# Splitting the mixers' weights a turn later and ending it earlier, with the mixers' parts in a new order

## The chip, the cores and the metric

The kernel runs on one core of a Trainium2 chip. The metric is the device time of one execution in microseconds (us); with several runs their median is taken. The profile and the trace come from one execution of their own. TensorE is called PE in the rows, its weight loads PEld, VectorE DVE, ScalarE ACT, GpSimd POOL and SyncE SP.

## What is computed

The kernel computes a model of two layers over 512 positions of width 1024, in float32. Each layer is a feed-forward block (FFN), a mixer of three kinds of heads, and a second FFN; a final norm ends it:

```python
for l in range(DEPTH):
    x = x + 0.5 * swiglu(rmsnorm(x, ffn1_norm[l]), ffn1_w_gate[l], ffn1_w_up[l], ffn1_w_down[l])
    h = rmsnorm(x, mix_norm[l])
    p_a, p_b, p_c = _split(h @ w_in[l], (A_IN, B_IN, C_IN))
    ...
    o_a = rwkv7_mixer(r, k, v, w_lo, a_lo, g_lo, ...)
    o_b = dsa_mixer(q_b, c_b, iq_b, ik_b, iw_b, ...)
    o_c = retention_mixer(q_c, k_c, v_c, g_c)
    x = x + jnp.concatenate([o_a, o_b, o_c], axis=-1) @ w_out[l]
    x = x + 0.5 * swiglu(rmsnorm(x, ffn2_norm[l]), ffn2_w_gate[l], ffn2_w_up[l], ffn2_w_down[l])
return rmsnorm(x, final_norm)
```

`rmsnorm` divides x by the root of its mean square and multiplies by a gain. `rwkv7_mixer` is a recurrence over time with six heads of 64, `dsa_mixer` an attention over the 128 keys that an index picks for each query, `retention_mixer` a chunked linear attention with four heads. The FFN's inner width is 2752, `w_in` has 3400 columns (3416 in the second layer).

## The kernel before

**The precision.** A float32 product is made of three matmuls in the rounded format fp32r: each operand is split into a high and a low part, and high times high, low times high and high times low are summed in PSUM (`mm3`, lines 846 to 851). For a weight tile (128 x up to 8 x 128) `_weights` issues a load on SP's queue into `raw` (L783), a cast to `hi` on ACT (L787) and a subtraction to `lo` on DVE (L788). There are two buffers each of `raw`, `hi` and `lo`.

**The FFN.** `ffn` (line 904) takes x transposed, in eight tiles `x` of 128 features x 512 positions that stay in SBUF. The norm makes `gxh` and `gxl` of each tile (x times the gain, split; L866 on ACT and L867 on DVE), its squares (L877 on ACT), adds them on DVE (L882 and L886) and takes the sum over the partitions with one matmul, `ms` (L888). 43 tiles of the gate and up weights follow (`gu_tile`, 24 matmuls each), and in three groups eight tiles each of the down weights (`down`); a group's `down` stands after the first pair of the next group, the last group's at the end. Each `down` tile ends with an addition to the tile of x on DVE (L976).

**The ahead splits.** The mixers' weights `win` and `wout` are split during the FFNs before them. `ahead` (L792) takes one granule of 128 x 4 x 128: a load on POOL's queue (`later`, L816), which is issued once the cast of the weight tile in hand is done; a cast on ACT (`ahh`, L798), a subtraction on DVE into the loaded tile (`ahr`, L800), and two writes to DRAM on POOL's queue (L802). Both tiles come from the eight buffers of tag "ds". The first FFN of layer 0 has 54 such granules, its second and the first of layer 1 have 35 each, the last FFN none. An FFN has 43 + 24 = 67 turns, one per weight tile, and `other` spreads the granules over turns 9 to 67. The first FFN of each layer also loads the small weights after its fifth pair.

**The mixer.** `mix` (line 997) does not issue its operations at once. It records them in a `Stage`, which places them with a list scheduler by the dependencies, the free buffers, its own costs and the numbers in `TUNE`: `BIAS` and `FACTOR` shift and scale the urgency of each stream of operations, `DENSE` and `STICK` are two numbers of PE's choice, and `ORDER` is the order in which the blocks are recorded (rw0 to rw2 are the recurrence's pairs of heads, idx and att the attention's index and body, ret the retention, lat the keys' latent). Operations are then issued in the order found, and PE, DVE, ACT and POOL keep it; all of them carry line 1027. The mixer begins with a norm like the FFN's; each projection (`in`, 24 matmuls from `gxh`, `gxl` and the split weight tile `w`, loaded on SP's queue) is multiplied by `rb`, the inverse root that comes from `ms`, when it leaves PSUM. The recurrence inverts a triangular matrix with chains of 32x32 matmuls (`W` and `dX`). The `out` matmuls with `wout` end the mixer.

**The end.** In the last FFN the last `down` is done for one half of the positions and then the other, and `final` makes a norm of each half.

Of the kernel before, what the change touches and what calls it, by code (L numbers as in the profile page):

```python
# [19 lines left out]
NGU = 43  # L20
# [495 lines left out]
class Net:  # L516
# [9 lines left out]
            BIAS={"norm": -574, "in:lo": 168, "evac:in:lo": 94, "in:idx": 189, "evac:in:idx": 62,  # L526
                  "win-ret:cg0": -436, "evac:win-ret:cg0": 25, "win-ret:cg1": 55,
                  "evac:win-ret:cg1": 178, "rw": -349, "win-idx:iq0": -144, "evac:win-idx:iq0":
                  1039, "win-idx:iq1": -369, "evac:win-idx:iq1": 721, "win-idx:iq2": -63,
                  "evac:win-idx:iq2": 407, "win-idx:iq3": -76, "evac:win-idx:iq3": 431, "idx": 5,  # L530
                  "topk:1": 36, "topk:2": -524, "topk:3": -79, "win-ret:cq0": -30,
                  "evac:win-ret:cq0": 94, "win-ret:ck0": 47, "evac:win-ret:ck0": 311, "win-ret:cq1":
                  296, "evac:win-ret:cq1": 290, "win-ret:ck1": 389, "evac:win-ret:ck1": -2,
                  "win-ret:cv0": -35, "evac:win-ret:cv0": 420, "win-ret:cv1": 268,
                  "evac:win-ret:cv1": 282, "ret:in": 349, "ret:mid": 178, "ret:y": -40, "win-rw:k0":
# [8 lines left out]
                  "win-att:c": -97, "evac:win-att:c": 442, "lat": 64, "win-att:q0": -245,  # L544
                  "evac:win-att:q0": 507, "win-att:q1": -183, "evac:win-att:q1": 818, "win-att:q2":
                  -395, "evac:win-att:q2": 472, "att:0": 150, "att:1": 59, "att:2": -126, "out:oc":
                  -460, "wout:oc": -1030, "out:oa": -141, "wout:oa": -708, "out:ob": -332,
                  "wout:ob": -306},
            FACTOR={"norm": 0.83, "in:lo": 0.22, "evac:in:lo": 1.3, "in:idx": 1.65, "evac:in:idx":
# [29 lines left out]
            RETPS="pd",  # L579
            OUTPS="pi",  # L580
            AHEAD=2,
            DENSE=3013,
            STICK=5,
        ),
        dict(
# [53 lines left out]
            RETPS="pd",  # L639
            OUTPS="pi",  # L640
            AHEAD=1,
            DENSE=2209,
            STICK=13.5,
        ),
    )
# [1265 lines left out]
```

## Time and profile before

| | us |
|---|---|
| median of 3 runs | 2237.72 (2233.5 to 2244.03) |
| the profiled execution's own time | 2234.96 |
| its span, first to last instruction | 2233.0 |
| PE busy in it | 2141.7 |
| first FFN of layer 0, to PE's last `dn` matmul | 373.3 |
| mixer of layer 0 | 373.3 to 764.3 |
| the two FFNs between the mixers | 764.3 to 1118.3 and 1118.3 to 1474.5 |
| mixer of layer 1 | 1474.5 to 1860.4 |
| last FFN and final norm | 1860.4 to 2233.0 |

A row of the profile names the line, the engine, the operation and the tiles it writes and reads. The brackets of a timeline row tell how long the engine had been idle before it and which instruction or DMA ended that. The granted clock is that of TensorE as a share of its full speed; its mean over the span is 0.987. A window's busy time for PE says how much of a stretch PE had a matmul running, whatever the clock.

### The profile page before, as it was taken

How to read it: one execution, taken by the hardware profiler on the slowest of the kernel's cores; microseconds unless marked ns; L12 is line 12 of the kernel's file. 1: busy time of each engine (PE TensorE's matmuls, PEld its weight loads, DVE VectorE, ACT ScalarE, POOL GpSimd, SP SyncE). 2: the span in 40 equal slices, each digit the busy share in tenths (PEclk: the TensorE clock that was granted, in tenths of full speed). 3: DMA queues.
4: the chain of work that ended last, by engine and by line, in shares of the span. 5: the costliest groups of instructions: out<-in, count | busy, mean ns of one | idle time of the engine just before them, and what ended most of it. 6: DMA issues, size and time to landing. Idle time of an engine off the chain costs nothing.

```text
span 2233.0 us, 34747 instructions
## 1 busy us (share of the span) xinstructions
PE 2141.7 (96%) x13896; PEld 1735.7 (78%) x13896; DVE 1252.6 (56%) x2150; ACT 853.0 (38%) x1416; POOL 320.3 (14%) x549
## 2 busy tenths in 40 slices
PE   8999998999999899999999999989999989999997
PEld 6887876777677688888878888868777867888887
DVE  5545455359885554454555454543788735434446
ACT  4423335432455332332443232433435544322225
POOL 0322223121110011111201111211201100000001
PEclk9999998999999999999999999999999999999999
DMA  4766667333310445555535555574522113233224
GB/s 136 250 225 223 219 229 265 104 132 130 101 43 22 141 146 173 188 182 186 186 133 186 183 185 188 168 238 174 169 90 73 31 57 120 95 98 100 96 85 151
DMA packets 112290, 329.44 MB, mean 148 GB/s; under 512 B 15632, under 2 KB 32160, under 8 KB 112128
## 3 DMA queue, kind: packets, MB, share of 16 engines
q1 hardware_dynamic: 81056, 225.31, 30.3%
q0 software_dynamic: 31072, 101.90, 13.8%
q8 instruction: 109, 1.79, 0.3%
q14 instruction: 53, 0.43, 0.1%
HBM read 252.97 MB, written 72.09 MB: 146 GB/s over the span
## 4 chain that ended last, share of the span: by engine, by line
PE 47%; issue 32%; POOL 8%; DMA 7%; DVE 3%; ACT 3%; SPq 0%; POOLq 0%; DVEq 0%; ACTq 0%
PE in L1027 11%; PE gu L849 6%; PE gu L851 6%; PE gu L850 6%; POOL win L802 4%; PE out L1027 3%; DMA w<-win 3%; POOL ahr L816 2%; PE dn L851 2%; PE dn L849 2%; PE dn L850 2%; DMA w<-wout 2%; PE W L1027 1%; PE S L1027 1%; DMA ahr<-win 1%
## 5 line engine op out<-in xcount | busy, mean ns | idle before, releaser
L849 PE MATMUL gu<-gxh,hi 128*128 128x512 f32 x1376 | 539.2, 392 | 15.3 <-ACT hi L787 15.3
L851 PE MATMUL gu<-gxh,lo 128*128 128x512 f32 x1376 | 539.1, 392 | 2.6 <-DVE lo L788 2.6
L850 PE MATMUL gu<-gxl,hi 128*128 128x512 f32 x1376 | 537.6, 391 | 0.0
L787 ACT CAST hi<-raw 128x1024 fp32r<-128x1024 f32 (+3 forms) x292 | 282.6, 975 | 478.6 <-PE gu L850 221.6
L788 DVE TENSOR_TENSOR lo<-raw,hi 128x1024 fp32r<-128x1024 f32 (+3 forms) x292 | 329.6, 1134 | 61.2 <-ACT hi L787 54.5
L849 PEld LDWEIGHTS gu<-gxh,hi 128*128 128x128 f32 x1376 | 259.9, 189 | 72.1 <-ACT hi L787 17.9
L851 PEld LDWEIGHTS gu<-gxh,lo 128*128 128x128 f32 x1376 | 259.4, 189 | 60.4 <-DVE lo L788 6.3
L850 PEld LDWEIGHTS gu<-gxl,hi 128*128 128x128 f32 x1376 | 259.7, 189 | 54.8 <-issue 0.7
L851 PE MATMUL dn<-hh,lo 128*128 128x512 f32 (+1 forms) x712 | 269.1, 379 | 2.8 <-DVE lo L788 2.4
L849 PE MATMUL dn<-hh,hi 128*128 128x512 f32 (+1 forms) x712 | 269.1, 379 | 1.6 <-ACT hi L787 1.6
L850 PE MATMUL dn<-hl,hi 128*128 128x512 f32 (+1 forms) x712 | 268.6, 377 | 0.1
L1027 PE MATMUL in<-gxh,w 128*128 128x512 f32 (+1 forms) x736 | 250.5, 414 | 13.8 <-DMA w<-win 7.0
L800 DVE TENSOR_TENSOR ahr<-ahr,ahh 128x512 fp32r<-128x512 f32 x124 | 85.8, 692 | 308.7 <-ACT ahh L798 308.5
L798 ACT CAST ahh<-ahr 128x512 fp32r<-128x512 f32 x124 | 77.0, 621 | 354.1 <-DMA ahr<-win 255.0
L1027 PEld LDWEIGHTS in<-gxh,w 128*128 128x128 f32 x736 | 136.4, 191 | 52.2 <-DMA w<-win 12.2
L851 PEld LDWEIGHTS dn<-hh,lo 128*128 128x128 f32 x712 | 133.8, 188 | 31.3 <-DVE lo L788 7.0
L849 PEld LDWEIGHTS dn<-hh,hi 128*128 128x128 f32 x712 | 133.8, 188 | 29.0 <-ACT hi L787 5.0
L850 PEld LDWEIGHTS dn<-hl,hi 128*128 128x128 f32 x712 | 133.9, 188 | 25.0 <-DVE hl L856 0.3
L1027 PE MATMUL in<-gxl,w 128*128 128x512 f32 (+1 forms) x368 | 137.6, 408 | 0.6 <-DVE gxl L1027 0.6
L976 DVE SCALAR_TENSOR_TENSOR x<-dn,x 128x512 f32<-128x512 f32 (+1 forms) x104 | 67.0, 647 | 112.9 <-PE dn L851 112.2
L946 DVE TENSOR_TENSOR h<-gu,rb 128x512 f32<-128x512 f32 x84 | 57.9, 689 | 117.0 <-PE gu L851 116.9
L941 DVE TENSOR_TENSOR t<-gu,rb 128x512 f32<-128x512 f32 (+1 forms) x88 | 60.7, 689 | 92.0 <-PE gu L851 91.4
(328 smaller groups left out, 2744.1 us busy)
## 6 DMA issues: line engine op xcount, KB each, us to landing
raw<-wgu SPq DMA_DIRECT2D x172, 512.0 KB, 3.7
w<-win SPq DMA_DIRECT2D x92, 512.0 KB, 4.4
raw<-wdn SPq DMA_DIRECT2D x64, 512.0 KB, 3.5
ahr<-win POOLq DMA_DIRECT2D x92, 256.0 KB, 3.2
win<-ahh POOLq DMA_DIRECT2D x92, 256.0 KB, 2.4
win<-ahr POOLq DMA_DIRECT2D x92, 256.0 KB, 2.5
w<-wout SPq DMA_DIRECT2D x64, 192.0 KB, 2.6
raw<-wdn SPq DMA_DIRECT2D x24, 384.0 KB, 4.2
```

The costliest lines, as they stand in the source:

```text
L787: self.cast = nc.scalar.copy(hi[:, k:e], raw[:, :e - k])
L788: nc.vector.tensor_sub(lo[:, k:e], raw[:, :e - k], hi[:, k:e].bitcast(F32))
L798: nc.scalar.copy(hi, raw)
L800: nc.vector.tensor_sub(lo, raw, hi.bitcast(F32))
L802: nc.gpsimd.dma_start(d[:, k:k + 4], t)
L849: mm(ps, hi[:, k, :], rh, start=start, stop=False)
L850: mm(ps, hi[:, k, :], rl, start=False, stop=False)
L851: mm(ps, lo[:, k, :], rh, start=False, stop=stop)
L941: nc.vector.tensor_mul(t[:rows], g[:rows], rb[:rows])
L946: nc.vector.tensor_mul(h[:rows], u[:rows], rb[:rows])
L976: nc.vector.scalar_tensor_tensor(out=x, in0=ps, scalar=0.5, in1=x, op0=ALU.mult, op1=ALU.add)
L1027: op.ins = getattr(getattr(self.nc, op.engine), name)(*args, **kw)
```

## The change

It has four parts.

1. **The ahead splits.** A turn no longer loads a granule and casts it. It casts, subtracts and writes the granule that an earlier turn loaded, and then issues the load of the next. The cast is made to follow the cast of the weight tile in hand. The granules are spread over turns 6 to 59 of 67 (`NGU + 2 * NC`), so that the last `down` of eight tiles has none; with 54 granules that is one in each turn, with 35 it is 0.65 a turn (0.59 before).
2. **The mixers' tables.** All numbers of `BIAS` and `FACTOR`, `DENSE` and `STICK` are others, and `ORDER` is another, in both layers.
3. **The start.** In the first FFN of layer 0 the cast of the second weight tile is made to follow the sixth `gxh`.
4. **The end.** In the final norm of each half the last square is not added on DVE; a second matmul adds it in PSUM.

```diff
             ...
-            ORDER=("idx", "ret", "rw0", "rw1", "rw2", "lat", "att"),
+            ORDER=("rw0", "idx", "rw1", "ret", "lat", "rw2", "att"),
             ...
-            DENSE=3013,
-            STICK=5,
+            DENSE=1603,
+            STICK=23.4,
             ...
-    def ahead(self, l, n, m, k):
+    def ahead(self, item=None):
         nc = self.nc
         with self.kind(3):
-            for k in (k,):
-                raw, hi = self.z("ahr", shape=(128, 4, 128), tag="ds"), self.z("ahh", F32R, (128, 4, 128), "ds")
-                self.later(raw, self.a[n][l, :, m, k:k + 4])
-                nc.scalar.copy(hi, raw)
+            if self.loaded:
+                raw, (l, n, m, k) = self.loaded
+                hi = self.z("ahh", F32R, (128, 4, 128), "ds")
+                self.follow(nc.scalar.copy(hi, raw), self.cast)
                 lo = raw.bitcast(F32R)
                 nc.vector.tensor_sub(lo, raw, hi.bitcast(F32))
                 for t, d in zip((hi.bitcast(F32), raw), self.parts[l][n, m]):
                     nc.gpsimd.dma_start(d[:, k:k + 4], t)
+                self.loaded = None
+            if item:
+                l, n, m, k = item
+                raw = self.z("ahr", shape=(128, 4, 128), tag="ds")
+                self.later(raw, self.a[n][l, :, m, k:k + 4])
+                self.loaded = raw, item
 ...
             ins = nc.scalar.activation(hi, self.x[c], AF.Copy, scale=g)
+            self.early.append(ins)
 ...
-    def rms(self, ts, after=None):
+    def rms(self, ts, after=None, apart=False):
             ...
-            else:
+            elif c < NC - 1 or not apart:
                 nc.vector.tensor_add(acc, acc, sq)
         ps = self.ps("ms")[:, ts]
-        nc.tensor.matmul(ps, self.c("onesd"), acc, start=True, stop=True)
+        nc.tensor.matmul(ps, self.c("onesd"), acc, start=True, stop=not apart)
+        if apart:
+            nc.tensor.matmul(ps, self.c("onesd"), sq, start=False, stop=True)
 ...
-        skip = 8
-        step, done = len(ahead) / (NGU + 3 * NC - skip), [-skip * len(ahead) / (NGU + 3 * NC - skip), 0]
+        skip, step, turn, done = 5, len(ahead) / (NGU + 2 * NC - 5), [0], [0]
+        assert step <= 1
 
         def other():
-            done[0] += step
-            while done[1] < round(done[0]):
-                self.ahead(*ahead[done[1]])
-                done[1] += 1
+            turn[0] += 1
+            if turn[0] > skip and done[0] < min(len(ahead), round((turn[0] - skip) * step)):
+                self.ahead(ahead[done[0]])
+                done[0] += 1
+            elif done[0] == len(ahead):
+                self.ahead()
 ...
             w = self.weights(wgu[l, :, m], 8)
+            if self.phase == 1 and m == 1:
+
+                self.follow(self.cast, self.early[5])
             other()
 ...
-                rbs.append(self.rms(ts))
+                rbs.append(self.rms(ts, apart=True))
```

Two further lines let a `wout` tile be left out of the ahead splits where `LATE` names it; it names none in either version, so they change nothing. Line numbers move by one (L787 is L788 after) to 17 (L1027 is L1044).

On ACT, at the border of the first FFN and the first mixer, the instructions stood like this (`hi` is the cast of a weight tile of the last `down`, `ahh` that of a granule, `sq` and `gxh` belong to the mixer's norm, `x_72` is the first tile of x and `x_74` the second):

```order
L787 CAST hi_2851<-raw_2849 128x768
L787 CAST hi_2883<-raw_2881 128x768
L798 CAST ahh_2856<-ahr_2855 128x512
L787 CAST hi_2915<-raw_2913 128x768
L798 CAST ahh_2888<-ahr_2887 128x512
L787 CAST hi_2947<-raw_2945 128x768
L798 CAST ahh_2920<-ahr_2919 128x512
L798 CAST ahh_2952<-ahr_2951 128x512
L1027 ACTIVATE sq_2993<-x_72 128x512
L1027 ACTIVATE gxh_2977<-x_72,vec 128x512
L1027 ACTIVATE sq_2994<-x_74 128x512
```

After the change:

```order
L788 CAST hi_2854<-raw_2852 128x768
L1044 ACTIVATE gxh_2977<-x_72,vec 128x512
L1044 ACTIVATE sq_2993<-x_72 128x512
L788 CAST hi_2879<-raw_2877 128x768
L788 CAST hi_2904<-raw_2902 128x768
L788 CAST hi_2929<-raw_2927 128x768
L788 CAST hi_2954<-raw_2952 128x768
L1044 ACTIVATE gxh_2979<-x_74,vec 128x512
L1044 ACTIVATE sq_2994<-x_74 128x512
L1044 ACTIVATE gxh_2981<-x_76,vec 128x512
L1044 ACTIVATE sq_2995<-x_76 128x512
```

The four granule casts are gone from this stretch, and the norm's first rows stand among the last weight casts.

On DVE at the same place, before (the addition to `x_86`, the last tile of x, and the norm's `gxl` and sums of squares):

```order
L800 TENSOR_TENSOR ahr_2951<-ahr_2951,ahh_2952 128x512
L976 SCALAR_TENSOR_TENSOR x_86<-dn_2958,x_86 128x512
L1027 SCALAR_TENSOR_TENSOR gxl_2978<-x_72,vec,gxh_2977 128x512
L1027 SCALAR_TENSOR_TENSOR sq_2993<-sq_2994,sq_2993 128x512
L1027 SCALAR_TENSOR_TENSOR gxl_2980<-x_74,vec,gxh_2979 128x512
L1027 TENSOR_TENSOR sq_2993<-sq_2993,sq_2995 128x512
```

and after it, from the sixth of the norm's rows on to its last sum:

```order
L1044 SCALAR_TENSOR_TENSOR gxl_2984<-x_78,vec,gxh_2983 128x512
L993 SCALAR_TENSOR_TENSOR x_86<-dn_2958,x_86 128x512
L1044 TENSOR_TENSOR sq_2993<-sq_2993,sq_2996 128x512
L1044 SCALAR_TENSOR_TENSOR gxl_2986<-x_80,vec,gxh_2985 128x512
L1044 TENSOR_TENSOR sq_2993<-sq_2993,sq_2997 128x512
L1044 SCALAR_TENSOR_TENSOR gxl_2988<-x_82,vec,gxh_2987 128x512
L1044 TENSOR_TENSOR sq_2993<-sq_2993,sq_2998 128x512
L1044 TENSOR_TENSOR sq_2993<-sq_2993,sq_2999 128x512
L1044 SCALAR_TENSOR_TENSOR gxl_2990<-x_84,vec,gxh_2989 128x512
L1044 TENSOR_TENSOR sq_2993<-sq_2993,sq_3000 128x512
```

Before, all of the norm's rows stand behind the addition to the last tile of x, which stands behind the split of a granule; after, six of them stand ahead of it and eight behind it up to the last sum.

On PE, in the inverse of layer 1's second recurrence, the rows after the change read like this (`dX` and `W` are the inverse's chains, `rsc` and `kt` small matmuls of the retention):

```order
L1044 MATMUL rsc_12923<-sw_12913,ck_2829_12894 128x128 x3
L1044 MATMUL dX_12854<-W_12851,X_12850 32x32 x32
L1044 MATMUL rsc_12923<-sw_12913,ck_2829_12894 128x128
L1044 MATMUL rsc_12925<-qz_12914,ck_2829_12894 128x128 x3
L1044 MATMUL W_12855<-X_12850,G_12833 32x32 x2
L1044 MATMUL W_12855<-X_12850,G_12834 32x32 x2
```

Before, the corresponding rows have projections (`in`) and products of the attention (`K`, `V`) between the chains:

```order
L1027 MATMUL K_13118<-cT_13040,wuk_10348 128x512
L1027 MATMUL K_13053<-cT_13040,wuk_10348 128x512
L1027 MATMUL dX_12828<-W_12825,X_12824 32x32 x32
L1027 MATMUL V_13060<-wuv_10350,cT_13040 128x128 x3
L1027 MATMUL W_12829<-X_12824,G_12807 32x32 x2
L1027 MATMUL W_12829<-X_12824,G_12808 32x32 x2
```

The chains are the same 32x32 matmuls; what lies between them has moved from 512-wide to 128-wide ones.

More of the change, by code (lines that the diff above doesn't have):

```diff
@@ L525 @@
         dict(
[L526 to L535, printed above, removed]
[8 rows of a table removed]
[L544 to L548, printed above, removed]
@@ L549 @@
-            FACTOR={"norm": 0.83, "in:lo": 0.22, "evac:in:lo": 1.3, "in:idx": 1.65, "evac:in:idx":
[18 rows of a table removed]
-                    1.84, "win-att:c": 0.2, "evac:win-att:c": 0.82, "lat": 0.2, "win-att:q0": 8.07,
-                    "evac:win-att:q0": 0.89, "win-att:q1": 1.57, "evac:win-att:q1": 2.62,
-                    "win-att:q2": 0.42, "evac:win-att:q2": 1.18, "att:0": 1.03, "att:1": 0.21,
-                    "att:2": 2.71, "out:oc": 0.2, "wout:oc": 2.02, "out:oa": 0.33, "wout:oa": 5.32,
-                    "out:ob": 0.2, "wout:ob": 3.44},
@@ L609 @@
-            FACTOR={"norm": 0.58, "in:lo": 7.83, "evac:in:lo": 0.23, "in:idx": 10.01, "evac:in:idx":
[18 rows of a table removed]
-                    1.68, "win-att:c": 0.61, "evac:win-att:c": 0.23, "lat": 2.22, "win-att:q0":
-                    1.89, "evac:win-att:q0": 0.23, "win-att:q1": 3.17, "evac:win-att:q1": 0.23,
-                    "win-att:q2": 1.73, "evac:win-att:q2": 0.23, "att:0": 2.76, "att:1": 1.73,
-                    "att:2": 1.01, "out:oc": 21.13, "wout:oc": 1.43, "out:oa": 0.2, "wout:oa": 4.45,
-                    "out:ob": 0.22, "wout:ob": 8.85},
@@ L633 @@
-            ORDER=("idx", "ret", "rw0", "rw1", "rw2", "lat", "att"),
+            BIAS={"norm": -1505, "in:lo": 403, "evac:in:lo": 1676, "in:idx": 354, "evac:in:idx":
[14 rows of a table added]
+                  550, "ret:mid": 436, "ret:y": 153, "win-att:c": 1, "evac:win-att:c": 151, "lat":
+                  455, "win-rw:k2": -527, "evac:win-rw:k2": 908, "win-rw:v2": -402,
+                  "evac:win-rw:v2": 3075, "win-rw:r2": -493, "evac:win-rw:r2": 2546, "rw2": 326,
+                  "rw2:in": -117, "rw2:gram": -19, "rw2:inv": -217, "rw2:state": 633, "rw2:y": 311,
+                  "win-att:q0": -165, "evac:win-att:q0": 1549, "win-att:q1": -434,
+                  "evac:win-att:q1": 1232, "win-att:q2": -312, "evac:win-att:q2": 1097, "att:0": 30,
+                  "att:1": -52, "att:2": -202, "out:oc": -992, "wout:oc": -1924, "out:oa": -161,
+                  "wout:oa": -1162, "out:ob": -834, "wout:ob": -1488},
@@ L634 @@
+            ORDER=("rw0", "idx", "rw1", "ret", "lat", "rw2", "att"),
             LATE=(),
@@ L641 @@
             AHEAD=1,
-            DENSE=2209,
-            STICK=13.5,
+            DENSE=2838,
+            STICK=113.3,
         ),
@@ L760, in setup @@
                        for n, k in (("win", NWIN), ("wout", NC)) for m in range(k)
-                       if n == "wout" or WIN_ORDER[m] not in self.TUNE[l]["LATE"]} for l in range(L)]
-        self.smalls = {}
+                       if (WIN_ORDER[m] if n == "win" else n) not in self.TUNE[l]["LATE"]} for l in range(L)]
+        self.smalls, self.loaded, self.early = {}, None, []
     def c(self, name):
@@ L1153, in _mix @@
             for m in range(NC):
-                w = self.split_weights(l, "wout", m, k0, kt)
+                if ("wout", m) in self.parts[l]:
+                    w = self.split_weights(l, "wout", m, k0, kt)
+                else:
+                    w = self.weights(a["wout"][l, :, m, k0:k0 + kt], kt)
                 if gi == 0:
```

50 lines of the change are left out of this document (38 added, 12 removed), and 103 rows, old and new, of tables (BIAS, FACTOR).

## The prediction

> **What bounds the kernel now.** I read the busy times first, then the stages by windows, then the waits and the timeline at the borders of the stages.
>
> ```profile
> span 2233.0 us, 34747 instructions
> PE 2141.7 (96%) x13896; PEld 1735.7 (78%) x13896; DVE 1252.6 (56%) x2150; ACT 853.0 (38%) x1416; POOL 320.3 (14%) x549
> ```
>
> TensorE (PE) is busy for 2141.7 of 2233.0 us: 91.3 us of idleness and the stretches at a low clock are all that a change of order can win. The windows say where they lie. The columns are start:end and length, then busy time and count on PE, PEld, DVE, ACT and POOL, the granted clock, the DMA share and GB/s.
>
> ```profile
> 7.00:113.00 106.00, 103.92 (x437) 83.71 (x438) 61.61 (x80) 46.99 (x66) 18.86 (x35) 1.00 0.57 191
> 157.00:246.00 89.00, 87.39 (x385) 71.68 (x384) 46.66 (x60) 33.20 (x45) 23.75 (x45) 1.00 0.67 220
> 373.30:764.30 391.00, 355.23 (x3769) 278.20 (x3770) 261.10 (x589) 170.59 (x363) 47.88 (x68) 0.97 0.31 103
> 764.30:1118.30 354.00, 353.36 (x1553) 290.81 (x1552) 182.45 (x227) 128.27 (x165) 57.29 (x106) 1.00 0.52 173
> 1474.50:1860.40 385.90, 357.75 (x3775) 281.74 (x3774) 254.41 (x595) 166.90 (x363) 45.63 (x64) 0.97 0.33 111
> ```
>
> The mixers (373.3 to 764.3 and 1474.5 to 1860.4) hold 391.00 − 355.23 = 35.8 us and 385.90 − 357.75 = 28.2 us of PE's idleness, 64 of 91. The second FFN of layer 0 holds 0.6 us though it splits 35 granules ahead; the first, with 54, loses 2.1 and 1.6 us in the two windows shown. So the FFNs are PE's own work, and what can move lies in the mixers, at their borders and in the first FFN.
>
> The border of the first FFN and the mixer, from the timeline (start, length, instruction, and in brackets the idle time before it and what ended it):
>
> ```profile
> 365.79 0.84 ACT L787 CAST hi<-raw 128x768 fp32r<-128x768 f32 x1
> 370.37 0.62 ACT L798 CAST ahh<-ahr 128x512 fp32r<-128x512 f32 x1 [3.75 <-DMA ahr<-wout]
> 374.66 0.62 ACT L798 CAST ahh<-ahr 128x512 fp32r<-128x512 f32 x1 [3.66 <-DMA ahr<-wout]
> 375.18 0.63 ACT L1027 ACTIVATE sq<-x 128x512 f32<-128x512 f32 x1
> ...
> 383.12 0.61 ACT L1027 ACTIVATE sq<-x 128x512 f32<-128x512 f32 x1
> ```
> ```profile
> 375.31 0.69 DVE L800 TENSOR_TENSOR ahr<-ahr,ahh 128x512 fp32r<-128x512 f32 x1 [2.99 <-ACT ahh L798]
> 375.92 0.68 DVE L976 SCALAR_TENSOR_TENSOR x<-dn,x 128x512 f32<-128x512 f32 x1
> 384.76 0.70 DVE L1027 TENSOR_TENSOR sq<-sq,sq 128x512 f32<-128x512 f32 x1
> ```
> ```profile
> 372.91 0.39 PE L851 MATMUL dn<-hh,lo 128*128 128x512 f32 x1
> 385.51 2.08 PE L1027 MATMUL ms<-sq,cst 128*128 128x512 f32 x2 [6.35 <-DVE sq L1027]
> ```
>
> PE ends its last `dn` matmul at 372.91 + 0.39 = 373.3. The `ms` matmul, without which no projection of the mixer can be evacuated, starts at 385.51, 12.2 us later. In between ACT stands idle twice, 3.75 and 3.66 us, for loads of the last two ahead granules; the norm's squares and casts, whose inputs but the last are long there, stand behind those casts and start at 375.18. DVE's last residual add has its matmul at 373.3 and starts at 375.92, behind the split of a granule. The other mixer's border has the same form:
>
> ```profile
> 1474.16 0.39 PE L851 MATMUL dn<-hh,lo 128*128 128x512 f32 x1
> 1474.74 0.62 ACT L798 CAST ahh<-ahr 128x512 fp32r<-128x512 f32 x1 [6.31 <-DMA ahr<-wout]
> 1486.12 2.08 PE L1027 MATMUL ms<-sq,cst 128*128 128x512 f32 x2 [5.86 <-DVE sq L1027]
> ```
>
> From 1474.55 to 1486.12 it takes 11.6 us. The clock drops there too:
>
> ```profile
> 377.80:391.50 13.70, 7.23 (x15) 4.63 (x15) 10.82 (x17) 9.35 (x16) 0.19 (x1) 0.50 0.54 191
> 1483.70:1490.60 6.90, 4.48 (x9) 2.89 (x10) 3.44 (x6) 2.58 (x5) 0.00 (x0) 0.51 0.47 183
> ```
>
> **The change, part by part.** *The borders.* No granule is cast in the last eight turns any more. ACT is free when it has made the last weight cast, at 365.79 + 0.84 = 366.6, with seven of eight x tiles finished or about to be; a pair of square and cast takes 1.13 us (the first square starts at 375.18, the eighth at 383.12), so seven pairs end by about 374.6 even where they wait for x. DVE has its last residual add ahead of eight operations: five additions of squares and three `gxl`, and that add waits for PE alone. It starts at about 373.4; it and the eight follow each other every 0.63 us (from 375.92 to 384.76, fourteen steps later, 8.84 us, 0.63 each). The last addition starts at 373.4 + 8 × 0.63 = 378.4 and `ms` 0.75 us later (385.51 − 384.76), at 379.2: 5.9 us behind PE's end in place of 12.2. That is −6.3. The other border has DVE's rows in the same order: 11.6 − 5.9 = −5.7. Together **−12.0**; what is late next is DVE's own row. The bounds are −3 together (if only the wait on the two loads counted half and DVE were held by late casts) and −18 (if the half-clock stretches went too). The same three projection matmuls stand ahead of `ms` before and after, so PE gains nothing else there.
>
> *The first FFN's stalls.*
>
> ```profile
> PE dn L851 <- DVE lo L788: 1.8, 3, 0.8
> PE gu L851 <- DVE lo L788: 1.6, 2, 0.9
> 181.54 0.62 ACT L798 CAST ahh<-ahr 128x512 fp32r<-128x512 f32 x1 [4.97 <-DMA ahr<-win]
> 185.41 0.50 PE L851 MATMUL gu<-gxh,lo 128*128 128x512 f32 x1 [0.90 <-DVE lo L788]
> ```
>
> The waits of PE from 40 to 341 us sum to 3.4 us, all on the weights' low half; the one at 185.41 follows a granule whose load ACT waited 4.97 us for, with DVE's split of it and the weight's low half behind it. After the change the granule cast is a turn old, and its row on ACT stands behind the weight cast. I take all of it, **−3.4** (0 to −3.5). One granule a turn instead of 54/59 raises the load on the DMA queues by 9% there; the windows show a DMA share of 0.67, so I charge nothing. In the added wait (a granule's cast behind the current weight cast) only POOL's writes and the granule's own buffers are queued, and no PE row reads them before the mixer.
>
> *The start.*
>
> ```profile
> 9.28 1.04 ACT L787 CAST hi<-raw 128x1024 fp32r<-128x1024 f32 x1 [2.38 <-DMA raw<-wgu]
> 10.38 0.80 PE L849 MATMUL gu<-gxh,hi 128*128 128x512 f32 x1 [1.37 <-ACT hi L787]
> ```
>
> ACT waits 2.38 us for the second weight tile with seven `gxh` casts behind it. Moved behind the sixth, these run while the tile lands. PE's idleness from 7 to 113 us is 2.1 us in all; I take **−1.5** (0 to −3).
>
> *The tail.*
>
> ```profile
> 2222.59 0.42 DVE L886 TENSOR_TENSOR sq<-sq,sq 128x256 f32<-128x256 f32 x1 [0.48 <-ACT sq L877]
> ```
>
> The last addition goes from the chain and a short matmul comes in: **−0.3** (−0.5 to +0.1).
>
> *The mixers' inside.* The numbers of the tables and the new order of the parts place all 1,750 PE rows of a mixer anew, with the same matmuls. Of the 35.8 and 28.2 us of idleness the borders hold their 12.2 and 11.6 us less the three projection matmuls ahead of `ms`, some 10 and 8; the ends, where the next FFN's first weight is waited for, hold 2.6 and 3.1 us:
>
> ```profile
> PE isc L1027 <- DVE iq L1027: 3.6, 4, 1.6
> PE in L1027 <- DMA w<-win: 3.3, 6, 0.9
> PE out L1027 <- DMA w<-wout: 2.9, 4, 1.3
> PE gu L849 <- ACT hi L787: 2.6, 1, 2.6
> PE out L1027 <- DMA w<-wout: 3.8, 3, 2.2
> PE gu L849 <- ACT hi L787: 3.1, 1, 3.1
> ```
>
> (The first four are of the first mixer from 391.5 on, the other two of the second from 1490.6 on.) That leaves 23 and 17 us inside, in many small waits. The new rows stretch the projections' matmuls, which wait for nothing but weights, further into the recurrences, and the output projection starts earlier and lies among attention's rows: more cover for just these waits. How much can't be read from an order. The bounds are −30 (three quarters of 40 gone) and +10 (new waits); I take 30%, **−12**.
>
> Against it stands that PE changes more often between 512-wide and smaller matmuls: counted in the rows, 691 times in both mixers before and 831 after. Their price comes from the mean length of a matmul.
>
> ```profile
> L849 PE MATMUL gu<-gxh,hi 128*128 128x512 f32 x1376 | 539.2, 392 | 15.3 <-ACT hi L787 15.3
> L1027 PE MATMUL in<-gxh,w 128*128 128x512 f32 (+1 forms) x736 | 250.5, 414 | 13.8 <-DMA w<-win 7.0
> ```
>
> A projection's matmul is 22 ns longer than an FFN's of the same shape. If all this is due to the changes, 22 ns on 736 + 368 of them is 24 us for 691 changes, 0.035 us each, and 140 more cost **+5** (0 to +5).
>
> Sum: −12.0 − 3.4 − 1.5 − 0.3 − 12 + 5 = −24.2. The profiled execution took 2234.96 us, so 2210.8. The median of the three runs, 2237.72, stands 2.8 above it, and the changed kernel will be told by a median too: 2213.6, so **2214**.
>
> **Rivals.** *The inside wins much more.* With −30 in place of −12, or the borders at −18, the time falls to 2190 to 2208; I put it at 2196. For it speaks that all of the order was placed anew; against it that 40 us lie in dozens of waits under 1.6 us.
>
> *The order gives back.* The freed borders are robust in the profile, the inside isn't: with +5 of new waits in place of −12 the time is 2231, and from 2226 to 2238 is this case's stretch.
>
> *Slower: the second layer's middle recurrence runs dry.* In the new order its 32x32 inverse has in some 30 us of PE time only seven projection matmuls between its chains. Before, the corresponding piece of another part was as poor, and one was rich:
>
> ```profile
> 1642.30:1658.50 16.20, 16.20 (x581) 11.77 (x580) 15.12 (x53) 0.99 (x2) 0.00 (x0) 1.00 0.08 27
> 1771.90:1790.80 18.90, 17.29 (x582) 14.00 (x581) 6.23 (x18) 3.98 (x9) 0.00 (x0) 0.73 0.01 3
> ```
>
> The poor one took 2.7 us more for the same count, at a clock of 0.73. At the clock of 0.50 and with waits at every step, 30 us become 50, and the fill that stood there is done later for its own 11 us: +31 against the −17 of borders, stalls and start, with the +5 some +19 or 2257. It decides for slower if the loss in that part passes 12 us, and by over 0.5% from 23; the 2.7 of the row speaks against it.
>
> *It doesn't do what it says.* If `ms` waits for something else, a late x load or the projection's weight, the borders keep 12 us and the time is 2226 at least; that is in the second rival.
>
> *The clock stays up at the borders.* The stretches at 0.50 and 0.51 held 7.23 and 4.48 us of PE's busy time; at full clock half, 5.9 us, would go: 2208. The pause of PE ahead of `ms` shrinks from 6.35 to some 4 us. But the profile shows a drop behind a pause of 2.6 us at the first mixer's end:
>
> ```profile
> 755.00:764.30 9.30, 6.71 (x23) 5.07 (x22) 4.53 (x6) 2.91 (x4) 0.00 (x0) 0.82 0.62 213
> ```
>
> So I don't take it. The Trainium skill, page "TensorE: Matmul & The Clock Gate", section "Part 1: The HAM clock gate", says that the clock falls to half after an idle window of about 3.4 us, and that these windows run free of the kernel. By that rule the pause left over would have to hold a whole window, and this rival would come true often; the 13.70 us at 0.50 are four such windows, which agrees, the drop behind 2.6 us does not.
>
> **How the numbers follow.** The forecast (2205 to 2226) has a chance of 0.45, the clock's rival (2208) 0.10, the much better inside (2196) 0.15, the order that gives back (2231) 0.22, the dry recurrence (2257) 0.08. A measurement of this kernel can tell about 0.5% from no change, 11 us: below 2226.5 is faster, above 2249 slower. Faster: 0.45 + 0.10 + 0.15 and a quarter of the fourth case, 0.75; slower 0.08; the same 0.17. The range leaves out the last case, the upper edge of the fourth and the lower edge of the third: 2194 to 2235.
>
> **What would show it.** In the changed profile `ms` should start 5 to 7 us behind the last `dn` matmul at both borders, no `ahh` row should stand between the last weight cast and the norm, and PE's waits on `lo` in the first FFN should be gone. If the mixers from the last `dn` to the first `gu` take 376 to 386 us (first) and 372 to 382 (second), the inside came as forecast; above 390 the new order has given back what the borders won. A stretch of clock under 0.8 in layer 1's middle recurrence would be the slower rival. What would make the forecast wrong is above all the inside of the mixers, of which I know rows and no times.

## The result, and the profile after

The changed kernel takes 2177.77 us (median of 4 runs, 2175.26 to 2178.81) against 2235.61 before (4 runs): a ratio of 0.9734, 95% interval 0.9705 to 0.9763. It is faster, as forecast, but by 58 us where 24 were forecast, and below the range of 2194 to 2235.

The page of the changed kernel, its first lines:

```profile
span 2173.5 us, 34793 instructions
PE 2115.9 (97%) x13900; PEld 1725.3 (79%) x13900; DVE 1252.3 (58%) x2148; ACT 846.6 (39%) x1416; POOL 316.8 (15%) x549
```

Of the 59.5 us by which the span is shorter, 33.7 are idle time of PE (91.3 before, 57.6 after). The other 25.8 are *busy* time (2141.7 to 2115.9), with the same matmuls but for the two that the final norm adds: what PE does goes faster, by the clock or by waits between matmuls that are too short to show as idle.

The windows of the stages, before and then after; a mixer is cut at the start of its `ms` matmul and ends at the next FFN's first matmul; the columns are those of the prediction's windows, and the three rows are the first FFN, the inside of mixer 0 and the inside of mixer 1:

```profile
7.00:373.30 366.30, 360.41 (x1554) 292.50 (x1554) 194.01 (x261) 140.14 (x189) 93.26 (x173) 1.00 0.66 219
385.50:760.20 374.70, 348.90 (x3755) 274.08 (x3755) 248.47 (x571) 158.90 (x344) 44.25 (x58) 0.99 0.29 96
1486.10:1860.40 374.30, 354.27 (x3767) 279.71 (x3767) 244.15 (x579) 157.21 (x346) 43.24 (x58) 0.97 0.31 104
```
```profile
6.90:365.60 358.70, 358.09 (x1556) 293.56 (x1556) 200.95 (x268) 146.34 (x204) 95.96 (x179) 1.00 0.71 230
372.00:729.30 357.30, 343.87 (x3763) 272.28 (x3764) 244.65 (x570) 158.79 (x343) 42.16 (x60) 0.99 0.31 101
1445.70:1802.10 356.40, 344.28 (x3767) 275.13 (x3767) 245.59 (x575) 156.71 (x342) 43.78 (x60) 0.99 0.33 110
```

| stage | before, us | after, us | change | forecast |
|---|---|---|---|---|
| first FFN, to the last `dn` | 366.3 | 358.7 | −7.6 | −4.9 |
| border of mixer 0, to `ms` | 12.2 | 6.4 | −5.8 | −6.3 |
| inside of mixer 0 | 374.7 | 357.3 | −17.4 | |
| FFN (1,0) and FFN (0,1) | 714.3 | 709.8 | −4.5 | 0 |
| border of mixer 1, to `ms` | 11.6 | 6.6 | −5.0 | −5.7 |
| inside of mixer 1 | 374.3 | 356.4 | −17.9 | |
| both insides | | | −35.3 | −7 |
| last FFN and final norm | 372.6 | 371.4 | −1.2 | −0.3 |

The insides alone hold 28 of the 35 us that the forecast missed by the profiles (59.5 less 24.2). Their idleness (length less PE's busy time) went from 25.8 to 13.4 and from 20.0 to 12.1 us, 20.3 together; their busy time went down by 5.0 and 10.0.

The border of mixer 0 after the change, on DVE and then on PE:

```profile
366.09 0.68 DVE L993 SCALAR_TENSOR_TENSOR x<-dn,x 128x512 f32<-128x512 f32 x1
...
371.27 0.68 DVE L1044 TENSOR_TENSOR sq<-sq,sq 128x512 f32<-128x512 f32 x1
```
```profile
365.42 0.39 PE L1044 MATMUL in<-gxl,w 128*128 128x512 f32 x1
367.20 0.50 PE L1044 MATMUL in<-gxh,w 128*128 128x512 f32 x1 [1.39 <-DMA w<-win]
367.54 0.40 PE L1044 MATMUL in<-gxl,w 128*128 128x512 f32 x1
372.01 2.07 PE L1044 MATMUL ms<-sq,cst 128*128 128x512 f32 x2 [4.08 <-DVE sq L1044]
```

The last `dn` ends at 365.6, DVE's last residual add comes at 366.09, its last sum of squares at 371.27 and `ms` at 372.01: DVE's own row is the chain, step by step as the prediction laid it out. No granule cast stands there.

ACT's waits from 20 us to the end of the first FFN, before and after:

```profile
ACT ahh L798 <- DMA ahr<-win: 109.2, 34, 6.9
ACT ahh L798 <- DMA ahr<-wout: 39.1, 13, 4.9
```
```profile
ACT hi L788 <- PE gu L858: 118.0, 39, 3.9
ACT hi L788 <- PE dn L858: 72.0, 20, 3.9
```

Before, ACT spent 148 us there waiting for the loads of granules, each wait ahead of a cast that PE might need. After, what ACT waits for is almost only that PE gives back a buffer: it runs ahead of PE all the way.

### The profile page after: what moved, and what is told of

It is laid out like the page before. It is cut to its first block, busy times and chain, and to the rows that moved or that the text cites. A ratio compares the mean times of both kernels' runs of the same rounds, so it can differ in the third digit from the quotient of the medians.

```text
span 2173.5 us, 34793 instructions
## 1 busy us (share of the span) xinstructions
PE 2115.9 (97%) x13900; PEld 1725.3 (79%) x13900; DVE 1252.3 (58%) x2148; ACT 846.6 (39%) x1416; POOL 316.8 (15%) x549
## 4 chain that ended last, share of the span: by engine, by line
PE 89%; DMA 4%; DVE 3%; ACT 2%; issue 1%; SPq 0%; POOL 0%; DVEq 0%; ACTq 0%; POOLq 0%
PE gu L857 14%; PE gu L859 14%; PE gu L858 14%; PE in L1044 11%; PE dn L857 7%; PE dn L859 7%; PE dn L858 7%; PE out L1044 4%; DMA w<-win 2%; PE po L1044 1%; PE W L1044 1%; PE S L1044 1%; PE dX L1044 1%; DMA w<-wout 1%; PE lg L1044 1%
## 5 line engine op out<-in xcount | busy, mean ns | idle before, releaser
L788 ACT CAST hi<-raw 128x1024 fp32r<-128x1024 f32 (+3 forms) x292 | 283.0, 976 | 829.4 <-PE gu L858 388.8
L1044 PE MATMUL in<-gxh,w 128*128 128x512 f32 (+1 forms) x736 | 245.0, 408 | 8.6 <-DMA w<-win 7.6
L1044 PEld LDWEIGHTS in<-gxh,w 128*128 128x128 f32 x736 | 136.2, 190 | 43.9 <-DMA w<-win 10.2
L1044 PE MATMUL in<-gxl,w 128*128 128x512 f32 (+1 forms) x368 | 135.8, 405 | 0.0
L824 POOL DMA_DIRECT2D ahr<-win x92 | 50.0, 543 | 581.7 <-ACT hi L788 564.5
L1044 PE MATMUL out<-oh,w 128*128 128x512 f32 x256 | 90.9, 419 | 3.8 <-DMA w<-wout 3.6
## 6 DMA issues: line engine op xcount, KB each, us to landing
raw<-wdn SPq DMA_DIRECT2D x24, 384.0 KB, 3.5
```

Of the source, the lines that this page charges most:

```text
L788: self.cast = nc.scalar.copy(hi[:, k:e], raw[:, :e - k])
L824: ins = self.nc.gpsimd.dma_start(out, src)
L1044: op.ins = getattr(getattr(self.nc, op.engine), name)(*args, **kw)
```

## The experiments

The time of the kernel before moves by some 20 us from run to run (2234.38 to 2254.11 in 19 runs on one chip), so ratios are to the runs of before on the same chip, and stages are read from the traces. Below, the time at half clock is that of the trace's clock records, which give the granted clock stretch by stretch, and the idleness of an inside is its length less PE's busy time.

### The parts alone

**tables_only.** The kernel before with the changed kernel's `TUNE`.

```diff
-            ORDER=("idx", "ret", "rw0", "rw1", "rw2", "lat", "att"),
+            ORDER=("rw0", "idx", "rw1", "ret", "lat", "rw2", "att"),
 (and all numbers of the two tables)
```

> The kernel before with the new tables and the new ORDER of both mixers, and nothing else. Theory A (the parts add up): the mixers' insides run as in the changed kernel, 353.5 and 351.1 us from the clock's rise behind ms to the next FFN's first matmul (368.7 and 369.8 before), while the granule casts still hold the borders and the first FFN still stalls: 2235.6 - 15.2 - 18.7 = 2202, from 2196 to 2208. Theory B (the rows of the new plan fit only a norm that is on time): behind the late norm the insides lose at least half of the gain, 2215 or more. My forecast's step (-7 for both insides together) would give 2229.

Measured: 2212.4 us, 0.9865 (0.9812 to 0.9918) of before, 30 us less. The insides:

```profile
389.70:753.20 363.50, 347.24 (x3763) 273.86 (x3764) 244.64 (x570) 158.77 (x343) 42.06 (x60) 0.99 0.31 99
1480.10:1834.00 353.90, 343.40 (x3767) 273.84 (x3767) 244.72 (x575) 156.56 (x342) 43.82 (x60) 0.99 0.33 110
```

363.5 and 353.9 us, 31.6 less together than before's 374.7 and 374.3 in the profiles, with the borders as late as before (12.7 and 10.6 us to `ms`). Theory A holds: the tables carry the insides, whatever the border does. The forecast's −7 falls. That this is no accident of two profiles is seen from all runs here: in the five with the old tables (before, ahead_only, ends_only, early_not_lagged and lagged_not_early) the insides take 374.7 to 384.8 us in mixer 0 and 370.6 to 376.6 in mixer 1, in the four with the new ones and nothing else moved in the mixers (after, tables_only, after_again, after_same_chip) 357.3 to 363.5 and 353.9 to 360.2.

**ahead_only.** The kernel before with the new `ahead` and `other`, as in the change.

```diff
-    def ahead(self, l, n, m, k):
+    def ahead(self, item=None):
 ...
-        skip = 8
+        skip, step, turn, done = 5, len(ahead) / (NGU + 2 * NC - 5), [0], [0]
 ...
```

> The kernel before with the new ahead splits alone (a turn later, and ended before the last eight turns). Theory A: the borders give -10 to -12, the first FFN -3.4 to -6, and the insides of the mixers nothing: 2217 to 2223; ms starts 6 to 8 us behind the last dn matmul. Rival (part of the insides' gain in the changed kernel came from the borders, by the clock and by weights that are loaded earlier): below 2214, with an inside of a mixer more than 3 us shorter than before.

Measured: 0.9892 (0.9851 to 0.9934), 24 us less, where 13 to 19 were expected; by the time alone it would be the rival. But the rival's second condition fails: the first FFN ends at 365.3 us, `ms` starts 4.6 and 6.4 us behind the last `dn`, and the insides are 383.5 and 374.7 us, no shorter than before. The profiled execution itself is only 13.9 us shorter than before's. So the borders and the FFN are this part's, the insides are not. The product of the two ratios is 0.976, at the upper edge of the whole change's interval: within their errors the parts add up.

**ends_only.** The edits of the start and of the final norm alone.

```diff
+            if self.phase == 1 and m == 1:
+                self.follow(self.cast, self.early[5])
 ...
-                rbs.append(self.rms(ts))
+                rbs.append(self.rms(ts, apart=True))
```

> The kernel before with the edits of the start and of the final norm alone. By the forecast's terms -1.5 and -0.3: 2234, hardly to be told from the 2235.6 before. Rival: the start is the larger part of the first FFN's 7.6 us (the clock also rises 2 us earlier there): -3 to -4, 2232. In the trace the second tile's wait of 1.37 us at 10.4 us should be gone, the first 432 matmuls should take 103.4 us as in the changed kernel (105.7 before) by the rival and about 104.3 by the forecast.

Measured: 1.0008 (0.9981 to 1.0035). In the trace the first 432 gate and up matmuls take 104.2 us (105.7 before), as the forecast had it, and the tail 10.9 us (11.4). The tail's 0.5 us stands in every profile with this edit and in none without. The start's 1.5 us is not shown to be the edit's: the four other profiles without it (tables_only, ahead_only, early_not_lagged, lagged_not_early) don't have before's wait of 1.37 us at 10.4 us either, and take 102.8 to 106.0 us there.

### Which half of the ahead part

**early_not_lagged.** The granules end before the last eight turns, but each is loaded and cast in the same turn.

```diff
 kernel before, and
-        skip = 8
 ...
+        skip, step, turn, done = 5, len(ahead) / (NGU + 2 * NC - 5), [0], [0]
 ...
+                self.ahead(*ahead[done[0]])
```

> The kernel before whose granules end before the last eight turns, as in the changed kernel, but are loaded and cast in the same turn as before. Theory A: the borders' gain comes from ending early: ms starts 6 to 8 us behind the last dn matmul and 10 to 12 us go, while the first FFN keeps its stalls on the weights' low half (3.4 us, perhaps more with one granule in each turn): 2223 to 2229. Rival: the lag is needed for the border too, since the last granules' loads still hold ACT among the last weight casts: 2230 to 2236.

Measured: 0.9960 (0.9942 to 0.9978). `ms` starts 4.6 and 6.4 us behind the last `dn`, so ending early does make the borders. But the first FFN takes until 381.2 us, 8 longer than before; PE's waits in it from 20 us on:

```profile
PE gu L851 <- DVE lo L788: 7.9, 9, 1.5
PE gu L849 <- ACT hi L787: 0.9, 3, 0.5
```

One granule in every turn without the lag costs PE 8.5 us of waits on `lo` (these 7.9, and 0.6 ahead of `dn` matmuls), more than double the 3.4 us that before's spread cost. The part of the expectation that let it stay at 3.4 was too low; the border's was right.

**lagged_not_early.** The lag, but granules to the end of the FFN.

```diff
 kernel before with the new ahead and other, but
+        skip, step, turn, done = 8, len(ahead) / (NGU + 3 * NC - 9), [0], [0]
```

> The kernel before whose granules are cast a turn after their load, but are spread to the end of the FFN as before (the last load in turn 66 of 67, its cast in turn 67). Theory A (the lag carries both the first FFN and the border, ending early adds little): first FFN some 366 us, ms 6 to 9 us behind the last dn matmul, 0.988 to 0.992 of before, as with both edits (0.989). Rival (ending early makes the border): first FFN some 366 us, but ms 10 us or more behind, 0.993 to 0.997.

Measured: 0.9911 (0.9887 to 0.9935). The first FFN ends at 366.4, so the lag alone takes its stalls away. `ms` starts 10.1 us behind in layer 0, where ACT still waits 3.82 us for the load of the last granule, ahead of the norm's first square, and 6.5 us behind in layer 1:

```profile
365.19 0.62 ACT L798 CAST ahh<-ahr 128x512 fp32r<-128x512 f32 x1 [3.82 <-DMA ahr<-wout]
365.72 0.63 ACT L1036 ACTIVATE sq<-x 128x512 f32<-128x512 f32 x1
```

The truth lies between the two expectations: the lag carries the FFN and one border, ending early the other.

### What in the tables does it

**after_old_numbers** and **after_old_order.** The changed kernel with the new `ORDER` and before's numbers, and with before's `ORDER` and the new numbers.

```diff
 after_old_numbers: BIAS, FACTOR, DENSE and STICK of before
 after_old_order:
-            ORDER=("rw0", "idx", "rw1", "ret", "lat", "rw2", "att"),
+            ORDER=("idx", "ret", "rw0", "rw1", "rw2", "lat", "att"),
```

> The changed kernel with the numbers of before in its tables, but the new ORDER. Theory O (the new order of the parts makes the insides' gain): the insides stay at 354 to 364 us, ratio 0.972 to 0.978. Theory N (the numbers make it): insides 374 to 384 us, ratio 0.986 to 0.992. Theory F (order and numbers are fitted to each other, either alone is worse than before): insides above 380 us, ratio above 0.990.

> The changed kernel with the ORDER of before, but the new numbers. Theory N: the insides stay at 354 to 364 us, ratio 0.972 to 0.978. Theory O: insides 374 to 384 us, ratio 0.986 to 0.992. Theory F: insides above 380 us, ratio above 0.990.

Measured: 1.0170 (1.0129 to 1.0212) and 1.0124 (1.0108 to 1.0139): both slower than before, though by less than 2%, and some 100 and 90 us behind the changed kernel. The insides of the first:

```profile
368.30:766.10 397.80, 359.11 (x3757) 278.76 (x3755) 245.53 (x568) 157.56 (x342) 43.28 (x60) 0.97 0.28 90
1486.30:1913.50 427.20, 378.28 (x3768) 298.12 (x3769) 254.28 (x580) 159.69 (x347) 43.52 (x60) 0.91 0.27 92
```

Neither the order nor the numbers make the gain alone: they are fitted to each other (theory F).

**after_no_dense** and **after_round5.** `DENSE = 0` in both layers; and every number of `BIAS` rounded to a multiple of five, as a control.

```diff
 after_no_dense:
-            DENSE=1603,
+            DENSE=0,
 ...
 after_round5:
-            BIAS={"norm": -336, "in:lo": -180, ...
+            BIAS={"norm": -335, "in:lo": -180, ...
```

> The changed kernel with DENSE = 0 in both mixers, so that the planner never prefers wide matmuls where PE has had little work. If the guard of the clock carries a part of the gain (theory C), the time at half clock inside the mixers rises from 12 us to over 30, the insides get 8 us or more longer each, ratio 0.980 or more. If it only holds idleness and order (rival), the time at half clock stays under 20 us and the ratio under 0.977.

> The changed kernel with every number of both BIAS tables rounded to a multiple of five, a control for how finely the numbers are fitted. If any shift of the plan costs (theory F in its fine form), the insides get 10 us or more longer together and the ratio to before is 0.979 or more; then the loss without DENSE says little of the clock. If the coarse structure carries the gain, the ratio stays at 0.971 to 0.977.

Measured: 0.9829 (0.9813 to 0.9844) and 0.9810 (0.9766 to 0.9854). Without `DENSE` the time at half clock rose to 33 us and the ratio past 0.980, as theory C wanted; but the idleness rose too, and rounding alone does the same. The mixers of after_no_dense, and then those of after_round5:

```profile
372.90:735.20 362.30, 347.92 (x3763) 274.40 (x3764) 246.39 (x572) 159.66 (x345) 42.13 (x60) 0.99 0.31 99
1451.60:1835.60 384.00, 354.97 (x3766) 277.80 (x3766) 250.37 (x579) 158.73 (x347) 43.56 (x60) 0.97 0.31 101
```
```profile
372.40:753.80 381.40, 355.64 (x3765) 279.31 (x3766) 248.83 (x576) 161.99 (x347) 43.30 (x60) 0.97 0.29 94
1470.30:1829.20 358.90, 345.13 (x3760) 273.50 (x3761) 244.41 (x573) 155.93 (x342) 43.39 (x60) 0.99 0.34 109
```

So after_no_dense says nothing of `DENSE` by itself. What both say: a plan next to the fitted one loses all of the gain in one mixer (384.0 and 381.4 us) and little or nothing in the other (362.3 and 358.9).

### The border and the clock

**after_again.** The changed kernel unaltered.

> The changed kernel unaltered, on the chip of this call, as the measure for the next two: 0.970 to 0.977 of before. Its trace shows how far the insides (357.3 and 356.3 us from ms to the next FFN's first matmul) and their time at half clock (4 and 9 us) repeat: within 6 us and 10 us.

Measured: 0.9716 (0.9680 to 0.9752), 2181.52 us; insides 360.0 and 360.2 us with 6 and 19 us at half clock. It repeats within the bounds expected, the second mixer's time at half clock just so.

**after_fill16.** Sixteen projection matmuls are taken ahead of `ms` in PE's row, of tiles already begun and with operands already issued; the other engines keep their rows.

```diff
+    FILL = 16
 ...
-        ops = stage.order()
+        ops = self.fill(stage.order(), self.FILL)
 ...
+    def fill(self, ops, n):
+        out = lambda op: op.parts[0][1][0].tensor.name
+        i = next(i for i, op in enumerate(ops) if op.engine == "tensor" and out(op).startswith("ms"))
+        head, seen, rest = ops[:i], set(ops[:i]), []
+        begun = {out(op) for op in head if op.engine == "tensor"}
+        for op in ops[i + 1:]:
+            if n and op.engine == "tensor" and out(op) in begun and all(d in seen for d in op.deps):
+                head.append(op)
+                seen.add(op)
+                n -= 1
+            else:
+                rest.append(op)
+        return head + [ops[i]] + rest
```

> The changed kernel with sixteen projection matmuls of each mixer moved ahead of ms in PE's row, of tiles already begun, so that PE has work while DVE adds the squares. If PE's wait for ms is still a cost of the border (theory W), ms starts within 1 us of where it did (6.4 and 6.6 us behind the last dn) with the sixteen done by then, the stretch from ms to the next FFN is 3 to 5 us shorter in each mixer, perhaps 3 more where the clock no longer drops: 0.992 to 0.997 of the changed kernel, 0.965 to 0.970 of before. Rival (the projections can't be evacuated before rb anyway, and PE only waits later for a free bank): within 0.2% of the changed kernel. Second rival: the loads of w are late, ms itself is held behind them by 3 us or more, and nothing is won.

Measured: 2172.24 us, 0.9676 (0.9637 to 0.9714) of before, 9.3 us or 0.43% less than after_again on the same chip; all six runs lie below all six of that. Theory W holds in its time, and in layer 1 in its border too. That border, on PE:

```profile
1442.96 1.07 PE L1060 MATMUL in<-gxh,w 128*128 128x512 f32 x4
1445.21 1.13 PE L1060 MATMUL ms<-sq,cst 128*128 128x512 f32 x2 [1.18 <-DVE sq L1060]
```

PE is busy up to 1.18 us before `ms`, and `ms` takes 1.13 us in place of 2.07: the clock is up. In layer 0 sixteen were too many; their weight came late there (PE waits 2.23 us for it) and `ms` starts 8.5 us behind the last `dn` (6.4 in the changed kernel), not within 1 us as expected.

**after_fill8_16** takes eight in layer 0.

```diff
-    FILL = 16
+    FILL = 8, 16
```

> As after_fill16, but with eight matmuls moved ahead of ms in layer 0 in place of sixteen, since there sixteen held ms up by 2 us (their weight lands 2 us behind the last dn). If the delayed ms cost anything, layer 0 gains 1 to 2 us on after_fill16: 0.994 to 0.996 of the changed kernel. If the moved matmuls are worth as much as ms, no difference to after_fill16: 0.995 to 0.997.

Measured: 2171.53 us, 0.9667 (0.9644 to 0.9689), beside the changed kernel's 2182.72 us on the same chip (after_same_chip, 0.9711, 0.9689 to 0.9733):

> The changed kernel unaltered, as the measure for the two others of this call: 0.970 to 0.976 of before.

The ratio to that, 0.995, is as good as that of after_fill16 (0.996): `ms` is back at 6.4 us in layer 0, and the mixer is no shorter for it. These two kernels beat both the kernel before and the changed one.

**after_warm.** Four matmuls of no use ahead of `ms`, which fill the same wait without doing any of the work. Only work is added.

```diff
+        old = self.x[0]
 ...
+                if op.engine == "tensor" and op.parts[0][1][0].tensor.name.startswith("ms"):
+                    for _ in range(4):
+                        self.nc.tensor.matmul(op.parts[0][1][0], self.c("onesd"), old, start=True, stop=True)
                 for name, args, kw in op.parts:
```

> The changed kernel with four float32 matmuls of no use (the ones matrix times the first tile of x, into the bank that ms then overwrites) ahead of ms in PE's row in both mixers: some 3.7 us of work in a wait of 5. Theory C (the clock at the border is a cost of its own): the two stretches at half clock behind ms, 6.8 us each, go or halve, each mixer is 1.7 to 3.4 us shorter from its last dn to the next FFN, 0.9965 to 0.9985 of the changed kernel. Rival (the clock doesn't matter there, PE waits for rb and for evacuations anyway): the stretches go and the time stays within 0.1%. Second rival: the extra matmuls hold ms up by 1 us or more and the time is 0.1% longer or worse.

Measured: 2178.28 us against 2182.72 on the same chip, 0.998. From the last `dn` to the next FFN, the changed kernel and then this one:

```profile
366.40:732.60 366.20, 347.50 (x3766) 274.12 (x3766) 251.57 (x581) 161.34 (x347) 42.14 (x60) 0.98 0.32 103
1443.50:1809.50 366.00, 349.93 (x3773) 279.35 (x3771) 251.48 (x585) 157.72 (x345) 43.66 (x60) 0.98 0.35 114
```
```profile
365.80:732.70 366.90, 349.30 (x3775) 274.33 (x3774) 250.51 (x580) 160.99 (x346) 42.04 (x60) 1.00 0.32 103
1442.40:1805.60 363.20, 350.10 (x3781) 278.15 (x3780) 251.54 (x586) 158.19 (x345) 43.61 (x60) 0.99 0.35 114
```

The two stretches at half clock behind `ms` are gone, the medians differ by 4.4 us and these stretches by 2.1 (2.8 in layer 1, −0.7 in layer 0). The runs of the two kernels overlap (2173 to 2184 and 2180 to 2185 us), so theory C is supported in size, not settled: some 2 to 4 of the 9 to 11 us that filling with useful matmuls brings would be the clock's. For the rest being the work that is done in the wait speaks that useless and useful filling leave the same time at half clock in the whole span (16.3 us in after_warm, 15.8 in after_fill8_16, 36.1 in after_same_chip), and yet their medians differ by 6.8 us.

## Why the prediction was right or wrong

**The borders: right.** "ms 5 to 7 us behind the last dn": 6.4 and 6.6. "That is −6.3" and "−5.7": −5.8 and −5.0; DVE's last add came 0.5 us behind PE's end, held by its own `gxl`, and the eight steps from it to the last sum took 0.65 us each in place of 0.63. Late next is what the prediction named, DVE's own row; after_fill16 shows that PE's wait behind it still cost some 9 us in both mixers together, the clock included.

**The first FFN: right on the stalls, low in its sum.** "−3.4" and "−1.5" were 4.9; measured −7.6. ahead_only alone ends the first FFN 8.0 us sooner than before, ends_only 0.8. Of the stage's 7.6 us, PE's idleness holds 5.3 (5.9 before, 0.6 after) and its busy time 2.3. PE's waits there, before and after (7.0 and 6.9 us of the waits on `hi` are the start of the kernel):

```profile
PE gu L849 <- ACT hi L787: 9.0, 4, 7.0
PE dn L851 <- DVE lo L788: 1.8, 3, 0.8
PE gu L851 <- DVE lo L788: 1.6, 2, 0.9
PE dn L849 <- ACT hi L787: 0.3, 1, 0.3
```
```profile
PE gu L857 <- ACT hi L788: 7.1, 2, 6.9
PE dn L857 <- ACT hi L788: 0.3, 1, 0.3
```

The 3.4 us on `lo` are gone, as forecast. The other 1.9 are on `hi`, and 1.37 of them are the wait at 10.4 us, which other profiles without the start's edit don't have: the −1.5 priced an accident of one execution, and that it came nearly out is luck. The 2.3 us of busy time had no term. Some 1 us of it may be the clock's, which first rises at 14.0 us in place of 16.0 (an estimate: half of the 2 us); the rest stays open.

The −4.5 of the two FFNs between the mixers had no term at all. PE's waits in the second of them, before:

```profile
PE gu L851 <- DVE lo L788: 1.0, 2, 0.7
PE gu L849 <- ACT hi L787: 0.6, 1, 0.6
```

ahead_only takes 354.1 us there in place of 356.5, and so does early_not_lagged, without the lag; lagged_not_early takes 355.2. So with 35 granules the new spread is enough, and the lag alone does a part. I had priced the stalls where they were densest only. The other 2.1 stand at the head of the first of the two FFNs and go with the mixer's tables (tables_only: 355.6 in place of 357.8): before, the last nine `out` matmuls of mixer 0 stand behind that FFN's first matmul, and after, none does. By its own last matmul mixer 0 has gained some 4 us more than its row in the table says.

**The mixers' insides: the step that failed.** "I take 30%, −12" and "140 more cost +5" gave −7; measured −35.3 (tables_only alone: −31.6). From the last `dn` to the next FFN the mixers take 363.8 and 362.9 us, where 376 to 386 and 372 to 382 were to show that the inside came as forecast. Three terms were wrong in it:

- The idleness fell by 20.3 of 45.8 us, 44%, where I took 30% of 40. The bound of −30 did hold it. Of the 20.3, 4.8 are the waits for the next FFN's first weight, which the forecast had set apart and given nothing (2.6 and 3.1 before, none and 0.9 after).
- The clock inside the mixers had no term. I priced it at the borders only, though the window quoted at 1771.9 us had 0.73 (and the one at 755 to 764, across the mixer's end, 0.82). By the clock records before's insides hold 9.4 and 19.2 us at half clock, after's 3.8 and 8.6: half of the difference, at most 8.1 us, is time.
- The changes between wide and narrow matmuls cost nothing that shows. Counted by width in the traces there are 548 in place of 498; the 691 and 831 of the prediction had put only projections and output matmuls on the wide side. The row that the price was read from mixes two shapes and has matmuls at half clock in it, and its mean fell from 414 to 408 ns with more changes (below). The busy time that the clock doesn't explain went down by 6.9 us (15.0 − 8.1), not up by 5. Why it went down the runs don't say; shorter waits between matmuls that don't show as idle are a guess. Why this plan has fewer waits than the old one stays open too: the runs show that order and numbers together do it, and not which rows.

```profile
L1044 PE MATMUL in<-gxh,w 128*128 128x512 f32 (+1 forms) x736 | 245.0, 408 | 8.6 <-DMA w<-win 7.6
```

**The rivals.** "The inside wins much more" came true, and further than its 2196. "The order gives back" did not. "The middle recurrence runs dry" did not in the profile of the changed kernel: that inverse's 661 matmuls take 19.1 us at a clock of 1.00.

```profile
1627.00:1646.10 19.10, 17.21 (x661) 15.30 (x661) 15.95 (x50) 1.85 (x6) 6.35 (x6) 1.00 0.11 33
```

My reading of the order there was right (hardly a projection between the chains), and it costs 1.9 us of idleness, not 31: small matmuls of the retention cover it nearly as well. Its part on the clock came true elsewhere: in both repeats of the changed kernel the clock falls to half for 6.8 us right behind this inverse, as here in after_again, which costs some 3.4 us more.

```profile
1629.10:1647.60 18.50, 17.28 (x663) 15.53 (x663) 16.08 (x52) 2.78 (x7) 6.22 (x5) 1.00 0.12 34
1647.60:1654.40 6.80, 6.80 (x32) 6.63 (x32) 3.07 (x10) 1.96 (x7) 0.37 (x1) 0.50 0.00 0
```

So the clock's part of this rival is real, and the changed kernel's own profile lacks it by luck.

"The clock stays up at the borders" did not come true by the change; the 4.08 us wait ahead of `ms` is followed by 6.8 us at half clock. after_warm shows that it can be had; its runs put it at 2 to 4 us, not 5.9.

## What to carry to other kernels

An engine that takes its rows in order waits for a load at the first row that needs it, with everything behind it. Loading one step ahead of the cast took 148 us of such waits from ACT for nothing but one more tile in flight; ending the background work eight tiles early helped where the next stage's first rows stand behind it, and without the lag, where it put a granule in every turn, it made the stage itself slower.

A schedule that was fitted as a whole has to be judged as a whole: either half of it (the order or the numbers) was worse than neither, and rounding its numbers cost one mixer 21 us. Price a new schedule by all that the old one loses (every idle stretch and every stretch at a low clock, here 46 and 14 us), and give it a wide range.

Before an order is fitted further, look for a wait that the fit has left: sixteen matmuls moved by hand into one wait of each mixer gave 9 us on top of it.

## What the runs showed of the hardware

The clock falls behind stretches in which PE was far from idle. In the kernel before it fell to half at 1777.3 and at 490.5 us by the clock records, in after_again at 1647.6; the 3.4 us ahead of each:

```profile
1773.90:1777.30 3.40, 2.67 (x127) 2.16 (x115) 1.03 (x3) 0.00 (x0) 0.00 (x0) 1.00 0.03 5
487.10:490.50 3.40, 1.78 (x7) 1.02 (x7) 1.76 (x4) 1.50 (x4) 0.00 (x0) 0.99 0.96 334
```
```profile
1644.20:1647.60 3.40, 3.00 (x77) 2.79 (x77) 2.40 (x11) 2.19 (x6) 0.00 (x0) 1.00 0.13 41
```

PE was busy for 2.67, 1.78 and 3.00 of 3.40 us, mostly with small matmuls in the first and the third, with seven wide ones in the second. Its longest pause in them was 0.7, 1.6 and 0.4 us. The Trainium skill, page "TensorE: Matmul & The Clock Gate", section "Part 1: The HAM clock gate", lets the clock fall in its table after an idle window of about 3.4 us. The length of the stretches agrees with that (3.41, 6.83, 10.24 and 13.65 us in the kernel before, multiples of 3.4); that the window has to be idle does not.

The spread of the kernel before from run to run goes with the clock: in its 19 runs on one chip the fastest (2234.38 us) had a mean clock of 0.989, the slowest (2254.11) 0.981. A loss of 0.008 of 2240 us is 18 us, and 20 were measured. It is not all: the runs at 0.984 among them lie between 2245.58 and 2253.66 us.
